# A decoder layer on one core: h's first quads asked for later, one more group with two k tiles by sevens, silu's product behind a split, diff heads closer together

## The chip, the cores and the metric

The kernel runs on one core of a Trainium2 chip, in float32. The metric is the device time of one execution in microseconds (us), the median of several runs. The engines are TensorE (PE; PEld is its weight load), VectorE (DVE), ScalarE (ACT), GpSimd (POOL) and SyncE (SP). SyncE and GpSimd issue DMAs.

## What is computed

One hybrid decoder layer on 256 tokens of width 2048: a half-step SwiGLU FFN, a mixer of two attentions (MLA with 8 heads, differential attention with 4 heads), and a second half-step FFN, each with a residual and a LayerNorm.

```python
def _swiglu(x, w_gate, w_up, w_down):
    return (jax.nn.silu(x @ w_gate) * (x @ w_up)) @ w_down
...
h = _layer_norm(ALPHA * h + 0.5 * _swiglu(h, ffn1_w_gate[l], ffn1_w_up[l], ffn1_w_down[l]), ln1_g[l], ln1_b[l])
mix = _mixer(h, positions, ...)
h = _layer_norm(ALPHA * h + mix, ln2_g[l], ln2_b[l])
h = _layer_norm(ALPHA * h + 0.5 * _swiglu(h, ffn2_w_gate[l], ffn2_w_up[l], ffn2_w_down[l]), ln3_g[l], ln3_b[l])
```

The FFN's inner width is 5632. Its inner activations, silu(gate) * up, are called h below.

## The kernel before

**Products.** A float32 product is made of three passes in the type fp32r. Each operand is split into a high part (a cast on ScalarE, L154) and a low part (a subtraction on VectorE, L155). `triple` (L207 to L210) multiplies high by high, high by low and low by high into one PSUM bank. Weights come by DMA as blocks of 128 x 1024 (two k tiles by 512 columns) on SyncE's queue and are split into pairs of the ring `wring`.

**Units and the order.** The work is a list of units, each with a load, a prep (adds and split) and the products (`unit`, `advance`). A load runs three units ahead of the prep, and preps run four units ahead of the products. `later(n, fn)` emits fn after n more units of products. This sets the order of the program's text. The order on each engine is then set by a scheduler at compile time. It may move an instruction ahead when its data and its buffer are there, it keeps the given order where `tc.issue_after(ins)` asks for it (an edge on the engine of `ins` alone, without a wait of its own), and buffers of one tag are handed out in turn. The activations of all stages share 41 slots of 4 KB per partition (tag "act"), and short-lived tiles share 6 (tag "tmp").

**Gate and up.** `ffn` first makes two column blocks with `project` (16 k tiles in 8 units of 12 matmuls each per block). Then ten groups follow (`Hybrid.group`, p = 1 to 10). A group makes two column blocks, that is one quad of h: 512 columns of h for both halves of the tokens. Inside a group, k tiles 0 to 7 are multiplied by a scheme with seven products in place of eight ("sevens": forms 1, 5, 6, 7, 2, 4, 3), where sums and differences of weight blocks are formed in place in the buffers `sraw` (L428 on VectorE, and L430 as an accumulating DMA on GpSimd). The other k tiles are plain units (L457). In a "wide" group k tiles 8 and 9 go by sevens too: each form has a third piece of 512 columns (buffers `eraw`, activation forms `xe` and `xm` of class `Extra`), and there are six plain units in place of eight:

```python
            elif wide:
                order = "15pp6p72q4q3q"
            elif seeded:
                order = "15pp6p7p2q4q3qq"
```

A digit is a form (three pieces when wide, two otherwise, of 6, 6 and 3 matmuls), and p or q is a plain unit of 12 matmuls. Groups 2 to 9 are wide, group 1 and group 10 are not. A wide group has 177 matmuls of 512 columns, a narrow one 180.

**From the group to h.** `sum_done` adds a snapshot to the bank (`gus`, L885), `half` calls silu on ScalarE (`sg`, L863) and multiplies it with up on VectorE (`hb`, L869), one unit later in the groups' later parts (`wait` is 1 there). Twelve units after a quad's second half, `put_h` transposes it in blocks of 32 (`blocks`, L715) and writes it to DRAM with four DMAs per token half on GpSimd's queue (`turn_out`, L717, into `hT`).

**Back from DRAM.** `get_h(q)` asks for a quad on GpSimd's queue (`hraw`, L893, two DMAs of 256 KB), and `split_h(q)` splits it into `h`. While group 10 is emitted, quads 3, 4 and 0 are asked for (units 3, 6 and 9 of it, counted from seven units before the end of group 9) and quads 3 and 4 are split (units 13 and 16). The down projection (`Sliced`) begins with quads 3 and 4. Quads 0 to 2 go through sevens there (`QuadForms`, tiles `xs` and `f`).

**The diff heads.** After the second hybrid run of the mixer, the four differential heads are spread over the units of the remaining projections. Each has four stages: scores, turn of the probabilities (L1103, L1105), values (L1248 to L1250), turn of the result (L1268). Stage i of head h is emitted at unit 2 + 6h + 3i + i // 3. Between them stand the column projections of q and k of the MLA heads, whose results are turned through DRAM (`turn_to_cols`, copies at L737).

Of the kernel before, what the change touches and what calls it, by code (L numbers as in the profile page):

```python
# [15 lines left out]
ALU = mybir.AluOpType  # L16
# [7 lines left out]
KF = DFF // P  # L24
# [35 lines left out]
def layer_kernel(ctx: ExitStack, tc: tile.TileContext, a: dict, out: bass.AP):  # L60
    nc = tc.nc
    V, S, GP, PE = nc.vector, nc.scalar, nc.gpsimd, nc.tensor
# [13 lines left out]
    def act_tile(shape, dt=F32, name="act"):  # L76
        return apool.tile(shape, dt, tag="act", name=nm(name), bufs=SLOTS)

    def tmp_tile(shape, name="tmp", dt=F32):
        return small.tile(shape, dt, tag="tmp", name=nm(name), bufs=6)  # L80
# [22 lines left out]
    def later(n, fn):  # L103
        uid[0] += 1
        heapq.heappush(todo, (step[0] + n, uid[0], fn))
# [42 lines left out]
            assert (k, b) in self.ready, (self.name, k, b)  # L148
            return self.tiles[k // 8, b][which][:, k % 8, :]

    cast, lows, fetched = [None], [None], [None]

    def split(hi, lo, src):
        cast[0] = S.copy(hi, src)  # L154
# [189 lines left out]
    def behind_split(n):  # L344
        return tc.issue_after(line[-n].ins) if len(line) >= n else nullcontext()
# [366 lines left out]
    def turn_out(row, to):  # L712

        t = tmp_tile([P, 512], "blocks")
        V.transpose(t, row)  # L715
        for i in range(4):
            nc.gpsimd.dma_start(to.rearrange("(g r) (i f) -> i r g f", g=4, i=4)[i],  # L717
                                t[32 * i:32 * (i + 1), :].rearrange("r (g f) -> r g f", g=4))

    def turned(v):  # L720
# [2 lines left out]
    def turn(row, use, wait, more):  # L723
        to = dram.tile([P, 512], F32, name=nm("turn"))
        turn_out(row, to)

        def back():
            t = tmp_tile([P, 512], "turned")
            nc.gpsimd.dma_start(t, to)
            later(more, lambda: use(turned(t)))  # L730
        later(wait, back)
# [120 lines left out]
    def ffn(n, x, wgu, wdn, residual, g, bt, each, first=None, between=None, nxt=None, cols=None, norm=None, pending=None):  # L852
        hb = {}
        hT = dram.tile([KF // 4, 2, P, 512], F32, name=f"hT{n}")

        def put_h(b, q):
            with behind_split(1):
                turn_out(hb[b, q], hT[q, b])

        def half(c, b, up, gate, wait=0):  # L860
            q = c // 2
            sg = tmp_tile([P, 256], "sg")
            S.activation(sg, gate, AF.Silu)  # L863
            if c % 2 == 0:
                hb[b, q] = tmp_tile([P, 512], "hb")
            o = (c % 2) * 256

            def product():
                V.tensor_tensor(out=hb[b, q][:, o:o + 256], in0=up, in1=sg, op=ALU.mult)  # L869
            if wait:  # L870
                later(wait, product)
            else:
                product()
            if c % 2 == 1:
                later(12, lambda: put_h(b, q))
# [4 lines left out]
        def sum_done(c, b, bank, snap, op):  # L880
            if snap is None:
                gu_done(c, b, bank)
                return
            t = tmp_tile([P, 512], "gus")
            V.tensor_tensor(out=t, in0=bank, in1=snap, op=op)  # L885
            half(c, b, t[:, 256:512], t[:, 0:256], 1)
# [2 lines left out]

        def get_h(q):  # L890
            raw = got[q] = act_tile([P, 2, 512], F32, "hraw")
            for b in range(2):
                nc.gpsimd.dma_start(raw[:, b, :], hT[q, b])  # L893

        def split_h(q):
            raw = got.pop(q)
            hq[q] = [act_tile([P, 2, 4, P], F32R, "h") for _ in range(2)]
            for b in range(2):
                split(*(t[:, b].rearrange("p k (i c) -> p k i c", i=4) for t in hq[q]), turned(raw[:, b, :]))
# [31 lines left out]
        for p in range(1, KF // 4):  # L931
            if p == KF // 4 - 1:
                for i, q in enumerate((3, 4, 0)):
                    later(3 + 3 * i, lambda q=q: get_h(q))
                later(13, lambda: split_h(3))
                later(16, lambda: split_h(4))
            hy.group(wgu[2 * p], wgu[2 * p + 1],
                     lambda n, b, bank, snap, op, p=p: sum_done(2 * p + n, b, bank, snap, op),
                     1 < p < KF // 4 - 1, p > 1)
        ln = LayerNorm(0.5, residual, g, bt, each, nxt, cols,  # L940
                       ((24, 26, 48, 50) if pending is None else (13, 14, 60, 62), (94, 97, 100, 103)),
                       35 if cols is None else None, pending, () if pending is None else (17, 32, 67, 82))
# [10 lines left out]
        for p in range(2):  # L953
# [30 lines left out]
            else:  # L984
                call(len(units) - 8, widen)
            down.run(wdn[2 * p], wdn[2 * p + 1], units, forms,
                     lambda m, b, bank, sign, p=p: ln.fold(2 * p + m, b, bank, sign),
                     lambda m, b, bank, p=p: ln.evac(2 * p + m, b, bank), calls, 8 * p)
# [119 lines left out]
    def mixer(x):  # L1108
# [105 lines left out]
        def gate(i, f, hook=None):  # L1214
            project((a["wgm"], a["wgd"])[i][f], x, KD, 512, lambda b, bank: keep_gate(i, f, b, bank), hook=hook)
# [57 lines left out]

        for h in range(DH):
            for i, f in enumerate(diff_head(h)):
                later(2 + 6 * h + 3 * i + i // 3, f)
        gate(1, 2, c_back)
        qT = [cols_proj(a["wuq"][c], cn, 4, "qT") for c in range(2)]
        qrT = act_tile([P, 4, T], F32, "qrT")
# [116 lines left out]

    h1 = Acts(KD, "h1", (0, 1))
    ffn(1, xq, a["gu1"], a["dn1"], a["x"], a["ln1_g"], a["ln1_b"], keep(0), first_tokens, second_tokens, h1, a["ln1_cols"])

    yq = mixer(h1)  # L1400
    h2 = Acts(KD, "h2", (0, 1, 2))
    ln = LayerNorm(1.0, res[0], a["ln2_g"], a["ln2_b"], keep(1), h2, a["ln2_cols"], ((1, 3, 11, 13), ()), 1,
# [94 lines left out]
```

## Time and profile before

| what | value |
|---|---|
| median of three runs | 1974.06 us (1972.81 to 1976.11) |
| the profiled execution | 1972.85 us, its span 1971.1 us |
| granted TensorE clock | 0.998 |
| ScalarE, the commonest group: casts of raw into wring, L154 | 467 instructions, 482.2 us |
| VectorE, the same for the low parts, L155 | 467 instructions, 559.1 us |
| VectorE, adds on sraw, L428 | 168 instructions, 200.2 us |
| GpSimd, writes of h, L717 | 176 instructions, 97.1 us |
| HBM | 246 GB/s over the span |

A row of a timeline gives the start in us from the span's start, the length in us, the engine, the line, the operation, the tiles (out<-in), the shape and the count; in brackets stands how long the engine was idle before it and what ended that. A row of waits gives the total in us, how often, and the longest. A row of the table by stretches gives the length of the stretch and each engine's busy time with the number of its instructions. A row of DMA issues gives the queue, the count, the size and the median us from issue to landing.

### The profile page before, as it was taken

The numbers are of one execution on the slowest core, as the hardware profiler recorded it, in microseconds if no ns is written. First come the engines' busy times: TensorE is split into PE (matmuls) and PEld (weight loads), VectorE is DVE, ScalarE is ACT, GpSimd is POOL, SyncE is SP. The second block draws the span as 40 slices with busy tenths as digits, with TensorE's granted clock in tenths as the row PEclk, the third lists the DMA queues.
The fourth block names the chain that finished last, engine by engine and source line by source line (L and its number), as shares of the span: only waits on it lengthen the run. The fifth ranks groups of instructions, "written<-read, shape, count | busy, mean of one in ns | idle before, by whom it ended". The sixth has DMA issues, their size and how long they took to land.

```text
span 1971.1 us, 25747 instructions
## 1 busy us (share of the span) xinstructions
PE 1955.1 (99%) x8784; PEld 1620.0 (82%) x8784; DVE 1773.5 (90%) x2175; ACT 1265.5 (64%) x1650; POOL 291.0 (15%) x503
## 2 busy tenths in 40 slices
PE   9999999999999999999999999999999999999997
PEld 7888888888888898888888888888888888888886
DVE  7999999999998879988976677789999999999986
ACT  6666767676655566666667765556676776665661
POOL 0112111122100010102223120001211112210000
PEclk9999999999999999999999999999999999999999
DMA  8978888777776666767667668578888878786763
GB/s 309 287 227 262 285 270 251 235 216 281 296 235 222 209 218 254 244 224 259 223 198 241 234 216 271 199 263 254 254 263 294 243 243 249 238 321 237 274 234 124
DMA packets 147478, 485.71 MB, mean 246 GB/s; under 512 B 20961, under 2 KB 21009, under 8 KB 147345
## 3 DMA queue, kind: packets, MB, share of 16 engines
q1 hardware_dynamic: 117360, 397.99, 58.2%
q0 software_dynamic: 29984, 86.07, 16.4%
q8 instruction: 69, 1.13, 0.2%
q14 instruction: 65, 0.52, 0.1%
HBM read 455.13 MB, written 28.84 MB: 246 GB/s over the span
## 4 chain that ended last, share of the span: by engine, by line
PE 95%; DVE 2%; DMA 1%; issue 1%; ACT 0%; SPq 0%; DVEq 0%; ACTq 0%
PE mm L209 30%; PE mm L210 30%; PE mm L208 30%; DVE wring L155 1%; PE tr L208 1%; PE tr L210 1%; PE tr L209 1%; DMA sraw<-in_gu_dram 1%; PE tr L671 0%; DVE sraw L428 0%; ACT wring L154 0%; DMA raw<-in_gu_dram 0%; PE tr L1228 0%; PE tr L1301 0%; PE tr L1303 0%
## 5 line engine op out<-in xcount | busy, mean ns | idle before, releaser
L154 ACT CAST wring<-raw 128x1024 fp32r<-128x1024 f32 (+2 forms) x467 | 482.2, 1038 | 296.5 <-PE mm L210 207.2
L155 DVE TENSOR_TENSOR wring<-raw,wring 128x1024 fp32r<-128x1024 f32 (+2 forms) x467 | 559.1, 1206 | 95.4 <-ACT wring L154 92.8
L154 ACT CAST wring<-sraw 128x1024 fp32r<-128x1024 f32 x436 | 454.8, 1054 | 230.2 <-DVE sraw L428 94.2
L155 DVE TENSOR_TENSOR wring<-sraw,wring 128x1024 fp32r<-128x1024 f32 x436 | 523.2, 1228 | 21.6 <-ACT wring L154 18.8
L210 PE MATMUL mm<-wring,h 128*128 128x512 f32 (+2 forms) x1248 | 480.2, 385 | 0.0
L208 PE MATMUL mm<-wring,h 128*128 128x512 f32 (+2 forms) x1248 | 480.2, 385 | 0.0
L209 PE MATMUL mm<-wring,h 128*128 128x512 f32 (+2 forms) x1248 | 479.8, 385 | 0.0
L209 PE MATMUL mm<-wring,xs 128*128 128x512 f32 x776 | 302.2, 389 | 1.3 <-DVE wring L155 1.3
L208 PE MATMUL mm<-wring,xs 128*128 128x512 f32 x776 | 302.2, 389 | 0.0
L210 PE MATMUL mm<-wring,xs 128*128 128x512 f32 x776 | 302.0, 389 | 0.0
L209 PEld LDWEIGHTS mm<-wring,h 128*128 128x128 f32 x1248 | 234.5, 188 | 46.8 <-DVE wring L155 0.7
L210 PEld LDWEIGHTS mm<-wring,h 128*128 128x128 f32 x1248 | 234.5, 188 | 46.5 <-DVE h L155 0.7
L208 PEld LDWEIGHTS mm<-wring,h 128*128 128x128 f32 x1248 | 234.4, 188 | 46.4 <-ACT h L154 0.6
L428 DVE TENSOR_TENSOR sraw<-sraw,sraw 128x1024 f32<-128x1024 f32 x168 | 200.2, 1229 | 3.5 <-DMA sraw<-in_wdv_dram 1.6
L209 PEld LDWEIGHTS mm<-wring,xs 128*128 128x128 f32 x776 | 145.7, 188 | 32.5 <-DVE wring L155 2.3
L208 PEld LDWEIGHTS mm<-wring,xs 128*128 128x128 f32 x776 | 145.7, 188 | 30.1
L210 PEld LDWEIGHTS mm<-wring,xs 128*128 128x128 f32 x776 | 145.7, 188 | 30.0
L717 POOL DMA_DIRECT2D hT<-blocks x176 | 97.1, 562 | 370.0 <-DVE blocks L715 368.2
L208 PE MATMUL mm<-wring,x 128*128 128x512 f32 x336 | 130.8, 390 | 0.8 <-ACT wring L154 0.8
L209 PE MATMUL mm<-wring,x 128*128 128x512 f32 x336 | 131.0, 390 | 0.5 <-DVE wring L155 0.5
L210 PE MATMUL mm<-wring,x 128*128 128x512 f32 x336 | 130.6, 389 | 0.0
L430 POOL DMA_DIRECT2D sraw<-in_gu_dram x40 | 35.6, 900 | 359.4 <-DVE sraw L428 309.0
(307 smaller groups left out, 2289.6 us busy)
## 6 DMA issues: line engine op xcount, KB each, us to landing
sraw<-in_gu_dram SPq DMA_DIRECT2D x160, 512.0 KB, 5.4
raw<-in_gu_dram SPq DMA_DIRECT2D x159, 512.0 KB, 4.7
raw<-in_dn_dram SPq DMA_DIRECT2D x140, 512.0 KB, 4.7
sraw<-in_gu_dram POOLq DMA_DIRECT2D x40, 512.0 KB, 6.9
sraw<-in_dn_dram SPq DMA_DIRECT2D x36, 512.0 KB, 5.6
hraw<-hT POOLq DMA_DIRECT2D x68, 256.0 KB, 6.2
eraw<-in_gu_dram SPq DMA_DIRECT2D x64, 256.0 KB, 6.0
raw<-in_w_out_dram SPq DMA_DIRECT2D x32, 512.0 KB, 4.3
```

Of the source, the lines that this page charges most:

```text
L154: cast[0] = S.copy(hi, src)
L155: lows[0] = V.tensor_tensor(out=lo, in0=src, in1=hi.bitcast(F32), op=ALU.subtract)
L208: PE.matmul(o, xh, wh, start=first, stop=False, skip_group_check=again)
L209: PE.matmul(o, xh, wl, start=False, stop=False, skip_group_check=again)
L210: PE.matmul(o, xl, wh, start=False, stop=last, skip_group_check=again)
L428: last = V.tensor_tensor(out=R[src][i], in0=R[src][i], in1=R[add[1]][i], op=ALU.add)
L430: nc.gpsimd.dma_start(R["12"][s], source("22", s), accum_op=ALU.add)
L717: nc.gpsimd.dma_start(to.rearrange("(g r) (i f) -> i r g f", g=4, i=4)[i], t[32 * i:32 * (i + 1), :].rearrange("r (g f) -> r g f", g=4))
```

## The change

Four places are touched. `turn_out` keeps its last DMA in `turned_out[0]`, and `get_h` puts its requests behind the one that is the last when the request is emitted, on GpSimd. The product of silu and up, where it is delayed by a unit, is put behind the split that is third from the end of those emitted so far, on VectorE. Group 10 becomes wide. The stages of diff head h are emitted at 2 + 5h + 3i + i // 3.

```diff
-    cast, lows, fetched = [None], [None], [None]
+    cast, lows, fetched, turned_out = [None], [None], [None], [None]
...
-            nc.gpsimd.dma_start(to.rearrange("(g r) (i f) -> i r g f", g=4, i=4)[i],
+            turned_out[0] = nc.gpsimd.dma_start(to.rearrange("(g r) (i f) -> i r g f", g=4, i=4)[i],
                                 t[32 * i:32 * (i + 1), :].rearrange("r (g f) -> r g f", g=4))
...
             def product():
-                V.tensor_tensor(out=hb[b, q][:, o:o + 256], in0=up, in1=sg, op=ALU.mult)
+                with behind_split(3) if wait else nullcontext():
+                    V.tensor_tensor(out=hb[b, q][:, o:o + 256], in0=up, in1=sg, op=ALU.mult)
...
         def get_h(q):
             raw = got[q] = act_tile([P, 2, 512], F32, "hraw")
-            for b in range(2):
-                nc.gpsimd.dma_start(raw[:, b, :], hT[q, b])
+            with tc.issue_after(turned_out[0].ins):
+                for b in range(2):
+                    nc.gpsimd.dma_start(raw[:, b, :], hT[q, b])
...
-                     1 < p < KF // 4 - 1, p > 1)
+                     p > 1, p > 1)
...
-                later(2 + 6 * h + 3 * i + i // 3, f)
+                later(2 + 5 * h + 3 * i + i // 3, f)
```

`behind_split(n)` is `tc.issue_after(line[-n].ins)`, where `line` holds the VectorE halves of the groups' splits in the order in which they were emitted.

## The prediction

> **What bounds the kernel now.** I read the page's head, the waits of TensorE, its timeline, the table by stretches, and last the timelines around TensorE's two stops inside the gate/up groups.
>
> ```profile
> span 1971.1 us, 25747 instructions
> ...
> PE 1955.1 (99%) x8784; PEld 1620.0 (82%) x8784; DVE 1773.5 (90%) x2175; ACT 1265.5 (64%) x1650; POOL 291.0 (15%) x503
> ```
>
> ```profile
> PE mm L209 <- DVE wring L155: 1.8, 4, 0.7
> PE tr L1248 <- ACT pt L1105: 1.1, 1, 1.1
> ...
> PE tr L1103 <- DVE p L1237: 0.2, 1, 0.2
> ```
>
> ```profile
> 229.81 0.39 PE L208 MATMUL mm<-wring,x 128*128 128x512 f32 x1
> ...
> 242.51 0.39 PE L210 MATMUL mm<-wring,xs 128*128 128x512 f32 x1
> ```
>
> TensorE is the bound. Its waits are a few us in all, and between the last two rows lie 57 products: 12.70/56 = 0.227 us from start to start. The 0.39 us of a record overlaps the next one, so a product that goes is worth 0.227. Whatever the change wins is products left out or one of these few waits. What it can lose is larger, because of the engine behind TensorE:
>
> ```profile
> core 0: us, PE busy (x) PEld busy (x) DVE busy (x) ACT busy (x) POOL busy (x), PEclk, DMA share, GB/s
> 217.90:258.90 41.00, 40.27 (x179) 33.04 (x177) 39.06 (x44) 27.47 (x36) 9.20 (x15) 1.00 0.83 271
> 258.90:299.00 40.10, 40.10 (x177) 33.12 (x178) 40.10 (x47) 27.82 (x37) 7.03 (x11) 1.00 0.84 256
> 419.40:460.20 40.80, 40.80 (x181) 33.80 (x181) 37.90 (x47) 26.78 (x35) 8.18 (x15) 1.00 0.73 248
> ```
>
> These are groups 5, 6 and 10 of the first FFN, nearly. In a wide group (6) VectorE is busy all the time; in the last, narrow one it has some 3 us free, ScalarE over a quarter everywhere. VectorE's steps, from the rows below (a record overlaps the next by 0.09): 1.13 us for 1024 columns, 0.60 for 512, 0.33 for 256, 1.22 for a pair of transposes.
>
> ```profile
> 254.27 0.68 DVE L885 TENSOR_TENSOR gus<-mm,snap 128x512 f32<-128x512 f32 x1
> 254.87 1.22 DVE L155 TENSOR_TENSOR wring<-sraw,wring 128x1024 fp32r<-128x1024 f32 x1
> 256.00 0.69 DVE L885 TENSOR_TENSOR gus<-mm,snap 128x512 f32<-128x512 f32 x1
> 256.60 0.42 DVE L869 TENSOR_TENSOR hb<-gus,sg 128x256 f32<-128x256 f32 x1
> ...
> 271.63 1.31 DVE L715 STREAM_TRANSPOSE blocks<-hb 128x512 f32<-128x512 f32 x2
> ```
>
> A wide group: 20 splits of 1024 and 7 of 512 (26.8), adds of 6 x 1.13 + 3 x 0.60 (8.6), three gus, four hb, two transposes (4.3): 39.7 us, against 177 x 0.227 = 40.1 of TensorE. The narrow one: 22 splits, six adds, the same rest: 36.0 against 180 x 0.227 = 40.8. So VectorE regains about 0.4 us per wide group and nearly 5 in the narrow one. What it loses in a wide group stays lost for long.
>
> Now the stop of group 6, and its twin in the second FFN:
>
> ```profile
> 237.20 2.17 POOL L893 DMA_DIRECT2D hraw<-hT  x4 [2.13 <-DMA hT<-blocks]
> ...
> 247.38 1.05 ACT L154 CAST wring<-sraw 128x1024 fp32r<-128x1024 f32 x1 [2.71 <-DMA sraw<-in_gu_dram]
> 248.78 0.42 DVE L869 TENSOR_TENSOR hb<-gus,sg 128x256 f32<-128x256 f32 x1 [1.91 <-ACT sg L863]
> 257.53 1.22 DVE L155 TENSOR_TENSOR wring<-sraw,wring 128x1024 fp32r<-128x1024 f32 x1
> 257.69 0.39 PE L208 MATMUL mm<-wring,xs 128*128 128x512 f32 x1
> 258.81 0.50 PE L209 MATMUL mm<-wring,xs 128*128 128x512 f32 x1 [0.73 <-DVE wring L155]
> ...
> 1531.68 0.39 PE L208 MATMUL mm<-wring,xs 128*128 128x512 f32 x1
> 1532.60 0.50 PE L209 MATMUL mm<-wring,xs 128*128 128x512 f32 x1 [0.53 <-DVE wring L155]
> ```
>
> The two quads 4 and 0 of h (four requests, 1 MB), wanted only by the down projection, are asked for in group 5. The next weights land late: median time to landing of sraw in 236 to 248 us, then in the same phase of the next group:
>
> ```profile
> sraw<-in_gu_dram SPq DMA_DIRECT2D x6, 512.0 KB, 7.0
> ...
> sraw<-in_gu_dram SPq DMA_DIRECT2D x6, 512.0 KB, 5.2
> ```
>
> ScalarE waits 2.71, VectorE 1.91, and ten us later TensorE loses 258.81 - 257.69 - 0.23 = 0.89 us (0.69 in the twin). Its undisturbed lead is read where a split ends and the L209 that needs it starts, at the two tightest units:
>
> ```profile
> 215.54 1.22 DVE L155 TENSOR_TENSOR wring<-sraw,wring 128x1024 fp32r<-128x1024 f32 x1
> 217.80 0.39 PE L209 MATMUL mm<-wring,xs 128*128 128x512 f32 x1
> ...
> 237.83 1.22 DVE L155 TENSOR_TENSOR wring<-sraw,wring 128x1024 fp32r<-128x1024 f32 x1
> 240.92 0.39 PE L209 MATMUL mm<-wring,xs 128*128 128x512 f32 x1
> ```
>
> 1.04 us at form 5, 1.87 at form 4. The first checks the account: 1.91 lost less 1.04 of lead is 0.87, and 0.89 was seen.
>
> **The change, part by part.** *Tenth group wide.* Three products fewer in each FFN: 6 x 0.227 = -1.36 us, sure. [...] The trace steps at 227, and that stands. The price lies on VectorE: 3.7 us more in that group (39.7 - 36.0). ScalarE gets 1.5 splits' worth more and has 14 us free; the requests change by 0.25 MB net, on POOL.
>
> *First quads of h.* At the place in the program where quads 3, 4 and 0 are asked for, the last write of h that has been emitted is that of quad 8 (quad 9's comes some 15 units later). So POOL issues all six requests, 1.5 MB at 0.54 us each, right behind the row at 392.83, from 397.2 on, just where the loads of the next group go out:
>
> ```profile
> 237.23 0.62 ACT L154 CAST h<-hraw 128x512 fp32r<-128x512 f32 x1
> ...
> 384.29 0.74 DVE L155 TENSOR_TENSOR h<-hraw,h 128x512 fp32r<-128x512 f32 x1
> 392.83 4.41 POOL L717 DMA_DIRECT2D hT<-blocks  x8 [14.49 <-DVE blocks L715]
> 398.87 4.63 SPq L420 DMA_DIRECT2D sraw<-in_gu_dram  x4
> ...
> 455.27 0.39 PE L208 MATMUL mm<-wring,h 128*128 128x512 f32 x1
> ```
>
> POOL itself has room, and h is wanted only at 455.27. The old stops go: -0.89 - 0.69 = -1.58. What is late next is the same thing one phase before the tenth group. The burst is half as large again, but starts some 2 us earlier against the weights, since these quads have long been written and need no wait as the 2.13 in the old row. I take the same loss on VectorE, 1.91; bounds 0 (all of it in idle queue time) and 3.0. Behind it stands the tenth group, now without VectorE's free 5 us, and there h's own splits fall: in the old trace ScalarE cast quad 3 at 237 and VectorE could do its half only at 384, when a slot of the last wide group came free; now the slots come free one group later, so all four of 0.60 (2.4 us) land in group 10, ahead of form 4.
>
> So in each FFN: at form 5, 1.91 - 1.04 = 0.9 us of stop. At form 4: what is still owed, 1.04, plus 2.4, less 0.3 regained, less the lead of 1.87: 1.3 us. Together 2.2, twice +4.4. Lower bound: no loss from the burst, 2.4 - 0.3 - 1.87 = 0.2, twice +0.4. Upper: 3.0 - 1.04 + 1.3 = 3.3, twice +6.6.
>
> *Product behind a split.* It goes behind a split two units ahead of the unit that was just multiplied; VectorE in a group is already four ahead by then (the row at 256.60 stands behind the split at 254.87). I cost it at 0; bounds -0.3 and +0.3, one hb of 0.33 on either side of a tight split.
>
> *Diff heads 5 apart.* The last head's scores are traced three units (8.2 us) earlier, its values also.
>
> ```profile
> 1047.44 1.47 PE L1228 MATMUL tr<-dkT,dqT 128*128 128x128 f32 x8
> ...
> 1064.76 1.01 DVE L1084 SCALAR_TENSOR_TENSOR st<-tr,bias 128x384 f32<-128x384 f32 x2
> 1076.22 0.62 ACT L737 COPY kT<-turned 128x512 f32<-128x512 f32 x1 [1.13 <-DMA turned<-turn]
> 1077.69 0.47 ACT L1105 COPY pt<-tr 128x384 f32<-128x384 f32 x1
> ```
>
> Its scores are done at 1049, its softmax starts 16 us later, because the six tmp buffers are handed out in program order and the turns of k stand before it. Then pt queues behind a copy that waits for a DMA, and TensorE waits 1.1 + 0.2. Ahead of the turns of k all of it is over before that copy: -1.3. Bounds: -1.6 (some switching goes too) and +1.3, when the copy's wait falls on a weight cast instead.
>
> **Sum.** -1.36 - 1.58 + 4.4 + 0 - 1.3 = +0.2 us. The profiled execution took 1972.85 around its span of 1971.1, the median of the three runs is 1974.06; 0.2 on the median gives 1974.3.
>
> **Rivals.** *All of it hides.* The early burst uses idle queue time, VectorE finds gaps for h's splits, and the heads give their better bound: -1.36 - 1.58 - 1.6 = -4.5: 1969.5. For it: group 4 had quad 3's two requests without a stop. Against it: the 39.7 of 40.1, and a lower bound above that still has a stop of 0.2.
>
> *VectorE is the bound through the tenth group* (slower). Besides h's 2.4, the first forms of quad 0 (0.33 + 4 x 0.33 + 2 x 0.60 = 2.9) are drawn ahead of form 4. With the burst at 3.0 a stop of 3.3 + 2.9 = 6.2 per FFN, 12.4 - 4.2 = +8.2: 1982.2; with the burst at 1.91, 5.1 twice, +6.0: 1980.0. It decides once what VectorE owes passes the 1.87 of lead. For it: no spare time in group 6; against it: those forms are traced behind the group's splits.
>
> *The queues share evenly.* [...] As a mechanism here: the loss grows with the bytes that stand beside the weights, 1.91 x 1.5 = 2.9, a stop of 3.2 per FFN, 6.4 - 4.2 = +2.2: 1976.2. The two landing times (7.0 and 5.2) agree in direction; the earlier start speaks against it.
>
> *The heads win nothing*, the wait moves to a weight cast: +0.2 + 1.3 = 1975.6, or 1976.9 with the bound.
>
> **How the numbers follow.** Chances: the sum 0.40, sharing 0.08, heads 0.10, all hidden 0.18, VectorE bound 0.24. About 0.2% (3.95 us) is what a measurement can tell: below 1970.1 only the hidden case, 0.18; above 1978.0 only the VectorE case, 0.24; within, 0.58. The forecast's own range is 1971.5 to 1977. The range for 8 in 10 takes in most of the hidden case and the lower half of the slow one: 1969.5 to 1980.5.
>
> **What would show it.** Right: no stop near 257 and 1531; hraw six in a row on POOL behind quad 8's write; TensorE waiting for L155 near 418 and again 20 to 25 us later; the h splits of quads 3 and 4 on VectorE inside the tenth group; no wait of L1248 for pt. Wrong: hraw behind quad 9's or 10's write, other tiles in the freed slots, a wait in the down projection, or kT late for the first MLA scores.

## The result and the profile after

The changed kernel takes 1982.51 us (median; 1979.53 to 1986.79), the kernel before beside it 1974.00 (1972.81 to 1976.11). The ratio is 1.0043, with a 95% interval of 1.0029 to 1.0056: slower by 8.5 us. The forecast was 1974.3, the range 1969.5 to 1980.5, so the time lies outside it. The profiled execution of the changed kernel took 1979.53 us around a span of 1977.8, 6.7 more than the span before. Behind L890 its line numbers are two higher (L1268 is L1270 now), and the product of silu and up stands on L870 (it was L869).

The page's head after, then the first waits of TensorE (total, how often, longest):

```profile
span 1977.8 us, 25757 instructions
...
PE 1955.3 (99%) x8778; PEld 1617.2 (82%) x8778; DVE 1780.6 (90%) x2191; ACT 1262.6 (64%) x1658; POOL 292.6 (15%) x505
```

```profile
PE mm L209 <- DVE wring L155: 5.0, 7, 1.0
PE tr L1270 <- DVE orow L1263: 2.6, 1, 2.6
PE tr L209 <- DVE wring L155: 1.5, 1, 1.5
```

Six matmuls fewer, and yet a longer span. The waits of L209 for a low part went from 1.8 to 5.0 + 1.5 (the second row is the same line with a bank of the tag `tr`, in the down projection). The 1.1 of L1248 for pt is gone, and 2.6 of L1270 for orow stands in its place.

GpSimd's timeline ahead of the tenth group of the first FFN; the median landing times of the weights that go out there, after and then before:

```profile
391.95 4.41 POOL L717 DMA_DIRECT2D hT<-blocks  x8 [14.89 <-DVE blocks L715]
396.36 3.23 POOL L895 DMA_DIRECT2D hraw<-hT  x6
```

```profile
sraw<-in_gu_dram SPq DMA_DIRECT2D x6, 512.0 KB, 8.8
hraw<-hT POOLq DMA_DIRECT2D x6, 256.0 KB, 8.1
```

```profile
sraw<-in_gu_dram SPq DMA_DIRECT2D x6, 512.0 KB, 5.0
```

The six requests stand in a row behind quad 8's write, as predicted, and the weights beside them land after 8.8 us in place of 5.0. What this does to ScalarE, then VectorE, then TensorE (the brackets hold the idle time before):

```profile
409.22 1.05 ACT L154 CAST wring<-sraw 128x1024 fp32r<-128x1024 f32 x1 [3.72 <-DMA sraw<-in_gu_dram]
...
536.09 0.62 ACT L154 CAST h<-hraw 128x512 fp32r<-128x512 f32 x1 [2.46 <-DMA hraw<-hT]
...
548.54 0.62 ACT L154 CAST h<-hraw 128x512 fp32r<-128x512 f32 x1 [4.33 <-DMA hraw<-hT]
```

```profile
410.62 0.42 DVE L870 TENSOR_TENSOR hb<-gus,sg 128x256 f32<-128x256 f32 x1 [3.33 <-ACT sg L863]
...
426.59 0.68 DVE L155 TENSOR_TENSOR h<-hraw,h 128x512 fp32r<-128x512 f32 x1
...
429.46 0.68 DVE L155 TENSOR_TENSOR h<-hraw,h 128x512 fp32r<-128x512 f32 x1
...
432.94 1.28 DVE L155 TENSOR_TENSOR h<-hraw,h 128x512 fp32r<-128x512 f32 x2
...
443.94 0.42 DVE L155 TENSOR_TENSOR xs<-hraw,xs 128x256 fp32r<-128x256 f32 x1
444.28 2.35 DVE L155 TENSOR_TENSOR wring<-sraw,wring 128x1024 fp32r<-128x1024 f32 x2
```

```profile
416.75 0.39 PE L208 MATMUL mm<-wring,xs 128*128 128x512 f32 x1
417.97 0.50 PE L209 MATMUL mm<-wring,xs 128*128 128x512 f32 x1 [0.83 <-DVE wring L155]
...
584.18 0.39 PE L208 MATMUL tr<-wring,xs 128*128 128x512 f32 x1
586.11 0.50 PE L209 MATMUL tr<-wring,xs 128*128 128x512 f32 x1 [1.54 <-DVE wring L155]
```

VectorE lost 3.33 us, more than the upper bound of 3.0, and took h's four splits (2.4 us at the prediction's 0.60 each) inside the tenth group, ahead of form 4, whose split is the row at 444.28. The stop at 584, 1.93 from start to start where 0.23 is due, was in no part of the sum. Its cause stands in ScalarE's rows at 536 and 549: it waits for quads of h that land late, with casts of weights behind it. In the kernel before, its longest wait for h there is this one:

```profile
530.33 0.62 ACT L154 CAST h<-hraw 128x512 fp32r<-128x512 f32 x1 [0.82 <-DMA hraw<-hT]
```

GpSimd's requests in the down projection, after and then before:

```profile
531.19 1.07 POOL L895 DMA_DIRECT2D hraw<-hT  x2 [11.30 <-DVE h L155]
544.36 2.12 POOL L895 DMA_DIRECT2D hraw<-hT  x4 [12.10 <-ACT wring L154]
```

```profile
534.06 1.07 POOL L893 DMA_DIRECT2D hraw<-hT  x2 [7.33 <-DVE h L155]
539.89 1.07 POOL L893 DMA_DIRECT2D hraw<-hT  x2 [4.76 <-PE mm L210]
```

A request can go out only when its slot of the tag "act" has been read for the last time. With the tenth group wide, these two pairs go out together at 544.36, where one went at 534 and one at 540 before. TensorE's work is 2.4 us behind by then, so that is 7.9 and 2.1 us later against the work, while the cast that needs the first of them stands in ScalarE's order at the same place. So what used to be early by a few us now comes just in time or late.

The table by stretches of groups 9 and 10 shows VectorE busy for 40.69 of 40.8 us in the tenth group, where it had some 3 us free:

```profile
378.90:419.90 41.00, 39.90 (x175) 32.39 (x173) 37.50 (x43) 26.73 (x35) 9.54 (x17) 1.00 0.84 278
419.90:460.70 40.80, 39.26 (x169) 31.32 (x170) 40.69 (x50) 29.39 (x39) 8.91 (x16) 1.00 0.64 190
```

In the mixer, TensorE's and ScalarE's timelines after, with VectorE's result of the last head after and before:

```profile
1069.19 0.59 PE L1252 MATMUL tr<-dv,pt 128*128 128x256 f32 x2
1083.94 0.44 PE L1270 MATMUL tr<-ident,orow 128*128 128x128 f32 x2 [2.55 <-DVE orow L1263]
```

```profile
1077.67 1.05 ACT L154 CAST wring<-raw 128x1024 fp32r<-128x1024 f32 x1 [1.97 <-DMA raw<-in_wbd_dram]
1078.62 0.38 ACT L1256 ACTIVATE junk<-tr 128x256 f32<-128x256 f32 x1
```

```profile
1083.40 0.88 DVE L1263 SCALAR_TENSOR_TENSOR orow<-tr,f,subg 128x256 f32<-128x256 f32 x2
```

```profile
1083.98 0.88 DVE L1261 SCALAR_TENSOR_TENSOR orow<-tr,f,subg 128x256 f32<-128x256 f32 x2
```

These times can't be compared as they stand, because the kernel after is 4.6 us behind by then: one and the same product of the projections starts at 998.26 after and at 993.70 before. Against the work, the last head's values are multiplied some 14 us earlier (1069 against 1079). The squares that come next on ScalarE start at 1078.62, behind casts of weights that wait for their DMA, and the result is there at 1083.40 against 1083.98, 5.1 us earlier against the work. TensorE comes to the turn at 1081.4 (1083.94 less its wait of 2.55) against 1084.6, which is 7.8 us earlier against the work. So the result moved less far than its consumer, and TensorE waits for the difference.

Stops of TensorE, as the time from the start of one product of 512 columns to the next less 0.227, summed by place where it is 0.15 or more. The last column is the second profile of the changed kernel (n_after_again, below). "Half clock" is a stretch in which the granted clock of TensorE is about 0.5; the rows of one, at 0.51, are shown at n_after_again.

| place | before | after | after, again |
|---|---|---|---|
| 257 and 1531 (sixth groups) | 1.58 | 0 | 0 |
| tenth group, first FFN | 0 | 3.44 | 4.21 |
| tenth group, second FFN | 0 | 2.12 | 2.61 |
| down projection, first FFN, 560 to 600 | 0 | 1.70 | 2.88, and 1.56 of half clock |
| last diff head, 1074 to 1086 | 1.63 | 2.71 | 2.36 |

With -1.36 for the products, the rows give +5.4 in the first profile (6.7 seen; 0.45 more stands at 950, a wait for dkT) and +9.1 in the second (10.0 seen).

### The profile page after: what moved, and what is told of

Its sections match the earlier page's. It is cut to its first block, busy times and chain, and to the rows that moved or that the text cites. A ratio compares the mean times of both kernels' runs of the same rounds, so it can differ in the third digit from the quotient of the medians.

```text
span 1977.8 us, 25757 instructions
## 1 busy us (share of the span) xinstructions
PE 1955.3 (99%) x8778; PEld 1617.2 (82%) x8778; DVE 1780.6 (90%) x2191; ACT 1262.6 (64%) x1658; POOL 292.6 (15%) x505
## 4 chain that ended last, share of the span: by engine, by line
PE 89%; DVE 5%; DMA 3%; issue 2%; ACT 1%; POOL 0%; SPq 0%; DVEq 0%; ACTq 0%; POOLq 0%
PE mm L209 28%; PE mm L210 28%; PE mm L208 28%; DVE wring L155 2%; DVE sraw L428 1%; DMA sraw<-in_gu_dram 1%; PE tr L209 1%; PE tr L210 1%; PE tr L208 1%; ACT wring L154 1%; PE tr L671 0%; DMA raw<-in_gu_dram 0%; DMA sraw<-in_wdk_dram 0%; DMA sraw<-in_wdv_dram 0%; DMA turn<-blocks 0%
## 5 line engine op out<-in xcount | busy, mean ns | idle before, releaser
L155 DVE TENSOR_TENSOR wring<-raw,wring 128x1024 fp32r<-128x1024 f32 (+2 forms) x463 | 552.2, 1201 | 94.9 <-ACT wring L154 93.2
L209 PE MATMUL mm<-wring,h 128*128 128x512 f32 (+2 forms) x1242 | 477.8, 385 | 0.0
L209 PE MATMUL mm<-wring,xs 128*128 128x512 f32 x776 | 303.1, 391 | 4.3 <-DVE wring L155 4.3
L209 PEld LDWEIGHTS mm<-wring,h 128*128 128x128 f32 x1242 | 233.3, 188 | 46.2 <-DVE wring L155 0.7
L209 PEld LDWEIGHTS mm<-wring,xs 128*128 128x128 f32 x776 | 145.6, 188 | 38.1 <-DVE wring L155 8.4
L209 PE MATMUL mm<-wring,x 128*128 128x512 f32 x330 | 128.8, 390 | 0.9 <-DVE wring L155 0.8
L208 PE MATMUL mm<-wring,x 128*128 128x512 f32 x330 | 128.5, 390 | 0.6 <-ACT wring L154 0.6
L210 PE MATMUL mm<-wring,x 128*128 128x512 f32 x330 | 128.3, 389 | 0.0
```

The lines of the kernel that those rows point to most:

```text
L155: lows[0] = V.tensor_tensor(out=lo, in0=src, in1=hi.bitcast(F32), op=ALU.subtract)
L208: PE.matmul(o, xh, wh, start=first, stop=False, skip_group_check=again)
L209: PE.matmul(o, xh, wl, start=False, stop=False, skip_group_check=again)
L210: PE.matmul(o, xl, wh, start=False, stop=last, skip_group_check=again)
```

## The experiments

Each ratio stands against the kernel before in the same comparison (medians 1972.98, 1973.38, 1973.41, 1973.30, 1973.30 in the five).

**The parts alone.** The edit on silu's product was not run by itself: VectorE's 2191 instructions stand in the same order in the profile of b_wide_tenth, which lacks it, and in that of abc_no_heads, which has it.

a_quads_late keeps only the edge on the requests:

```diff
+            with tc.issue_after(turned_out[0].ins):
```

> The kernel before with the requests for h's first quads behind the last write alone (narrow tenth group, heads 6 apart). Theory (VectorE's free time decides): the stops near 257 and 1531 us go (-1.6); the burst now stands ahead of the narrow tenth group, where VectorE has nearly 5 us free, so at most a stop of 1 us stays at its start and none later: 1972 to 1974 us. Rival (the burst alone costs what it cost, or more, wherever it lands): stops of 1 to 2 us in each FFN at the start of the tenth group, 1974 to 1977. Second rival (slots): the later quads of h are asked for too late in the down projection, and a stop appears there of 1 to 2 us.

b_wide_tenth keeps only the wide group:

```diff
-                     1 < p < KF // 4 - 1, p > 1)
+                     p > 1, p > 1)
```

> The kernel before with the wide tenth group alone (early requests for h, heads 6 apart). Theory (VectorE): six products fewer (-1.4), the old stops stay, and the tenth group, with 3.7 us more on VectorE and the splits of two quads of h, stops TensorE late in the group by 1 to 2 us per FFN: 1974 to 1977 us. Rival (the slots held one group longer push the requests of the later quads, and ScalarE waits for them in the down projection): a stop in the down projection of about 1.7 us in the first FFN, as in the changed kernel near 584 us.

d_heads_5 keeps only the heads:

```diff
-                later(2 + 6 * h + 3 * i + i // 3, f)
+                later(2 + 5 * h + 3 * i + i // 3, f)
```

> The kernel before with the diff heads 5 units apart alone. Theory (the last head's result is paced by the six tmp buffers, whatever its place in the program): the stop moves from the values (1.1 us at L1248) to the turn of the result (2.6 us), plus small ones: +2 us in the span, 1975.5 to 1977 us. Rival (the longer stop also lowers the granted clock in some executions): the runs scatter upward by 2 to 6 us more and their mean clock is 0.996 to 0.997 instead of 0.998.

abc_no_heads is the whole change without that last edit:

```diff
-                later(2 + 5 * h + 3 * i + i // 3, f)
+                later(2 + 6 * h + 3 * i + i // 3, f)
```

> The changed kernel with the heads back at 6 units. Theory: the FFN part alone, -1.6 (old stops) -1.4 (products) +5.6 (stops in the tenth groups) +1.7 (down projection) = +4.3 in the span, 1977.5 to 1979.5 us as a median, with stops of 1.0, 1.2 and 1.0 us in the first FFN's tenth group and 1.0 and 1.0 in the second's. Rival (clock): if the scatter of the changed kernel up to 1986.8 us comes from the mixer's long stop, this one scatters like the kernel before; if it comes from the stops in the FFN, it scatters like the changed one.

| kernel | median | ratio (95%) | stops in its profile |
|---|---|---|---|
| a_quads_late | 1974.52 | 1.0007 (0.9998 to 1.0016) | none at 257, 1531; 1.73 at 416, 1.01 at 1691; 0.61 at 1788 |
| b_wide_tenth | 1977.53 | 1.0018 (1.0007 to 1.0029) | 1.18 at 257, 0.81 at 1538; 0.68 at 442 and at 1723; 2.87 at 581 to 582, then half clock; 2.03 at 1081, then half clock |
| d_heads_5 | 1973.58 | 0.9997 (0.9988 to 1.0006) | 1.51 at 256 to 258, 1.18 at 1534; 3.37 at the last head's turn, then half clock |
| abc_no_heads | 1982.18 | 1.0037 (1.0023 to 1.0051) | 3.57 and 2.15 in the tenth groups; 3.70 at 563 to 586 |

The heads have no share in the loss that can be measured; the edge and the wide group together have nearly all of it, and more together (+9.2 in the medians, +7.3 by the ratio) than one by one (+1.5 and +4.6, by the ratios +1.4 and +3.6), though by the intervals that last difference could be chance. Of the four medians only that of a_quads_late lies where an expectation had it (that of its rival); b_wide_tenth and abc_no_heads are slower than expected, d_heads_5 is faster. The edge does what it says in one place and gives it back in another: the stop moves from 257 to 416 and gets larger.

The stop in the first FFN's down projection comes with the wide group, with the edge or without, and so do the late requests: two pairs go out together in b_wide_tenth, apart in a_quads_late. b, then a:

```profile
542.68 2.12 POOL L893 DMA_DIRECT2D hraw<-hT  x4 [12.81 <-ACT wring L154]
```

```profile
535.77 1.06 POOL L894 DMA_DIRECT2D hraw<-hT  x2 [8.44 <-DVE h L155]
540.76 1.06 POOL L894 DMA_DIRECT2D hraw<-hT  x2 [3.93 <-PE mm L210]
```

In the second FFN the edge alone has a smaller one, the 0.61 at 1788; ScalarE waits 4.99 us for h at 1767 there.

**The down projection.** e_h_split_late takes abc_no_heads and splits each quad of h three units later; the requests stay where they are in the program.

```diff
-                call(first_use, lambda q=q: split_h(q))
+                call(first_use + 3, lambda q=q: split_h(q))
```

> The changed kernel without the heads' edit, and in the down projection each quad of h is split three units (8.2 us) later than it was, while it is asked for at the same unit. Theory (requests for h that come just in time): in the kernel without the heads' edit ScalarE stood 3.18, 0.82 and 4.75 us at its casts of h near 538 and 551, with casts of weights behind them; three units later the data is there, these waits fall under 1 us in all, the stops of TensorE at 585 to 586 (0.74 and 2.10) are gone, and the median falls from 1982.2 to between 1978.5 and 1980.5. Rival (VectorE still owes from the tenth group, and the casts of h only show it): the waits go but a stop of 2 to 3 us stays between 560 and 600, and the median stays within 1 us of 1982.2.

It took 1977.93, 1.0029 (1.0018 to 1.0040). No stop over 0.15 between 455 and 680; ScalarE's longest wait at h's casts from 528 on:

```profile
531.82 0.62 ACT L154 CAST h<-hraw 128x512 fp32r<-128x512 f32 x1 [0.78 <-DVE h L155]
```

The theory held for the stop: the place at which ScalarE, whose casts of weights stand behind it in order, waits for h is what stops TensorE 40 us later. Its worth is less sure: 3.70 in the profiles, 4.3 by the medians, 1.6 by the ratios, with intervals that overlap; the next pair sharpens it.

**The tenth group.** f_group_split_late takes abc_no_heads and emits the two splits there 12 units later, past form 4.

```diff
-                later(13, lambda: split_h(3))
-                later(16, lambda: split_h(4))
+                later(25, lambda: split_h(3))
+                later(28, lambda: split_h(4))
```

> The changed kernel without the heads' edit, and the splits of quads 3 and 4 inside the tenth group are emitted 12 units later, so that VectorE has one of the four halves ahead of form 4 instead of four. Theory (VectorE's debt): 3 x 0.60 = 1.8 us less stand ahead of form 4, so the stops at 444 (0.95) and 1724 (0.96) fall under 0.2 each, those at 416 to 419 and 1699 (burst of requests) stay at 1.0 to 2.5, and the median falls by 1.5 to 2.0, from 1982.2 to 1980.2 to 1980.7, if the down projection takes the 1.8 us. Rival (the debt only moves): the stops at 444 and 1724 go, but 1 to 2 us of new stops appear within 25 us behind them or the one at 585 grows by as much; median within 1 us of 1982.2.

It took 1981.79, 1.0043 (1.0030 to 1.0055): the rival's time. The stops of 0.95 at 444 and 0.96 at 1724 are gone, and the down projection has one of 0.38 and one of 2.10, here TensorE's two rows, with half clock behind them:

```profile
583.42 0.50 PE L208 MATMUL tr<-wring,xs 128*128 128x512 f32 x1 [0.22 <-ACT wring L154]
...
585.74 0.50 PE L209 MATMUL tr<-wring,xs 128*128 128x512 f32 x1 [1.82 <-DVE wring L155]
```

The rival's mechanism is not what the profile shows, though: the stops in the down projection did not grow, they came to 2.48 where abc_no_heads has 3.70, with 0.62 more at 1756 in the second FFN. Over both FFNs the stops are 2.7 us less. Two stretches of 3.4 us at half clock, the one behind 2.10 here (0.53) and one behind 2.49 at 1082 in the mixer (0.51), took that back; the profile of abc_no_heads has none. So whether VectorE's debt from the tenth group is handed on stays open.

ef_both_late has both edits.

> The changed kernel without the heads' edit, with h's splits later in the down projection (three units) and inside the tenth group (12 units). Theory (two debts on VectorE, one after the other: the tenth group's, and that of requests that come just in time): with the second paid, what the first hands on no longer meets a stop, so the stops at 444 (0.94) and 1720 (0.96) go and none comes back at 580 to 590; those of the six requests at once (416 to 419: 2.45; 1693 to 1695: 1.0 to 1.7) stay. From 1977.9 with the down projection alone to 1975.7 to 1976.5. Rival (VectorE is the bound from the tenth group through the down projection, so every stop taken out comes back): a stop of 1 to 3 us between 455 and 600, median 1977.5 or more.

1975.98, 1.0015 (1.0006 to 1.0023), as the theory has it. Against f alone, whose interval begins at 1.0030, the later split in the down projection is worth 5.8 us. That includes the half clock in f. With the splits late in both places no stop is left in the first FFN behind 428. What is left are those of the six requests at once:

```profile
417.94 0.50 PE L209 MATMUL mm<-wring,xs 128*128 128x512 f32 x1 [1.21 <-DVE wring L155]
420.61 0.50 PE L209 MATMUL mm<-wring,xs 128*128 128x512 f32 x1 [1.02 <-DVE wring L155]
...
1695.59 0.50 PE L209 MATMUL mm<-wring,xs 128*128 128x512 f32 x1 [1.01 <-DVE wring L155]
```

**The requests.** g_requests_spread is the kernel before with an edge for each early quad; `written[q]` holds the last write of quad q.

```diff
+        behind_write = {3: 5, 4: 6, 0: 8}
...
-            for b in range(2):
-                nc.gpsimd.dma_start(raw[:, b, :], hT[q, b])
+            w = written.get(behind_write.get(q))
+            with tc.issue_after(w.ins) if w is not None else nullcontext():
+                for b in range(2):
+                    nc.gpsimd.dma_start(raw[:, b, :], hT[q, b])
```

> The kernel before, with one thing changed: quad 3's two requests stand behind the last write of quad 5, quad 4's behind that of quad 6, quad 0's behind that of quad 8 (on GpSimd), so no more than two stand together, in groups six, seven and nine. Theory (the stop comes from four or more requests at once): none of the stops at 257 (0.89) and 1531 (0.69) of the kernel before, none at 416 and 1691 of the kernel with six at once (1.39 and 0.66), and the median falls by 1.2 to 1.6 us against the kernel before. Rival (every request costs the weights its bytes wherever it stands): three smaller stops per FFN, 1.6 us or more in all; median within 0.5 us of the kernel before.

1972.52, 0.9994 (0.9985 to 1.0003). GpSimd asks two at a time, and there is no stop of 0.15 or more from 15 to 680 us and from 1300 to 1950:

```profile
275.28 1.10 POOL L899 DMA_DIRECT2D hraw<-hT  x2 [0.30 <-issue]
...
315.68 1.11 POOL L899 DMA_DIRECT2D hraw<-hT  x2 [0.59 <-ACT snap L386]
...
395.60 1.10 POOL L899 DMA_DIRECT2D hraw<-hT  x2
```

The profile is the theory's; the median fell by 0.9, less than the 1.2 to 1.6 expected, and its interval takes in no change. That fewer than four requests bring no stop is not so in every execution, as p_narrow_again shows below.

**The heads.** h_last_turn_late is d_heads_5 with the last head's fourth stage three units later.

```diff
-                later(2 + 5 * h + 3 * i + i // 3, f)
+                later(2 + 5 * h + 3 * i + i // 3 + (3 if h == 3 and i == 3 else 0), f)
```

> The kernel before with the heads five units apart, and the turn of the last head's result three units later; in TensorE's order it then stands six products (1.4 us) later and in one piece. Theory (the head's result is ready no earlier than before, because its squares stand behind casts of weights whose loads were issued late, so TensorE's wait is only a matter of where the turn stands): the wait of 3.2 us at the turn shrinks by 1.3 to 1.4 to about 1.9, nothing else moves, median 1972.0 to 1972.6 (heads five apart alone: 1973.6). Rival (the split of that result is wanted right behind the turn): the wait moves to the first product that uses it, 3 us in all stay, median 1973.1 to 1974.1.

1970.59, 0.9988 (0.9980 to 0.9997), better than expected. The wait of 3.2 us is 0.50 in the profile, where 1.9 was expected:

```profile
1079.84 0.83 PE L1268 MATMUL tr<-ident,orow 128*128 128x128 f32 x4 [0.50 <-DVE orow L1261]
```

So the wait was a matter of where the turn stood. Two things in the expectation need a correction. The result is ready some 4.5 us earlier than in the kernel before already in d_heads_5 (1079.62 against 1083.98, with the work nearly level), only the turn had moved further. And the heads' own gain in this profile is about 1 us (a stop of 0.66 where the kernel before has 1.63); the stops of the sixth groups, which the edit doesn't touch, happen to be 0.27 in place of 1.58. The wait is not gone either: in the six profiles of the repaired kernels below the stop at this turn is 0.40 to 1.70. m_after_last_turn_late makes the same edit on the changed kernel.

> The changed kernel with the last head's result turned three units later (six products in TensorE's order). Theory (the wait of 2.6 us is only a matter of where the turn stands, and a stop of over 2 us can also cost a stretch at half clock): the stop at the last turn falls from 2.7 to under 1 us, and the median from 1982.5 to 1979 to 1980.5. Rival (the changed kernel's median is set by its FFNs alone): less than 1 us better than 1982.5.

1979.14, 1.0039 (1.0025 to 1.0052). In the medians that is 3.4 less than the change, by the ratios (1.0043 to 1.0039) 0.8, with intervals that overlap; the wait at the last turn is 0.3 in its profile, as the theory has it, and how much of the change's time it was stays unsure.

**What the median has over the first profile.** n_after_again is the changed kernel, for a second profile.

> The changed kernel again, for a second profile. Theory (half clock after long stops): the time is 1981 to 1985, with at least one stretch of 3.4 us at about half the granted clock, behind the stop near 584 or the one near 1081, each worth some 1.7 us, and the same stops as in the first profile within 0.5 us. Rival (other stops that come and go): clock at 1.0 throughout, and stops of 1 us or more at places where the first profile has none.

It took 1982.89 around 1981.1, with the stops at the same places, and the theory's half clock. TensorE's rows, and the table by stretches (its last three columns are the granted clock, the DMA share and GB/s):

```profile
585.77 0.50 PE L208 MATMUL tr<-wring,xs 128*128 128x512 f32 x1 [0.61 <-ACT wring L154]
588.10 0.79 PE L209 MATMUL tr<-wring,xs 128*128 128x512 f32 x1 [1.83 <-DVE wring L155]
588.69 0.63 PE L210 MATMUL tr<-wring,xs 128*128 128x512 f32 x1
589.12 0.63 PE L208 MATMUL tr<-wring,xs 128*128 128x512 f32 x1
```

```profile
584.40:587.80 3.40, 1.26 (x5) 0.48 (x3) 3.40 (x4) 3.13 (x4) 0.00 (x0) 1.00 0.50 177
587.80:591.20 3.40, 3.10 (x7) 2.48 (x8) 3.40 (x4) 0.76 (x1) 0.00 (x0) 0.51 0.86 243
```

Behind a stop of 2.10 the products step at 0.43 us, not 0.227, for 3.4 us: 1.56 us lost on top. Of the six executions behind the median, the one of the first profile has a mean clock of 0.998 (1979.53 us), three have 0.997 (1981.55, 1981.55, 1983.46) and two 0.996 (1983.94, 1986.79). One such stretch takes 3.4 x 0.49 / 1981 = 0.0008 off the mean, which fits one or two of them in the longer executions.

**A version that beats both.** i_spread_wide_late is the kernel before with the tenth group wide, the requests spread as in g, and both edits of ef. k_spread_wide_late_heads adds the heads of h. gh_spread_heads has the edits of g and h alone, the tenth group narrow.

> The kernel before with the tenth group wide and all three repairs: the early requests spread (two at a time behind the last writes of quads 5, 6 and 8), h's splits later in the tenth group and in the down projection. Heads as before. Theory (the three causes are the requests that stand together, h's splits ahead of form 4, and the splits of h in the down projection): no stop over 0.3 us from 200 to 640 and from 1500 to 1950, the six products are won, so 0.89 + 0.69 + 1.36 less than the kernel before at most: median 1970.2 to 1971.2 (0.9984 to 0.9989). Rival (VectorE has no room for a tenth wide group at all): stops of 1 to 3 us in the tenth group or behind it, median 1972.5 to 1975.

> The same with the heads five apart and the last head's result turned six products later. If the parts add up: 1970.7 less the 1.5 to 2.8 that the heads won alone, median 1967.9 to 1969.2 (0.9972 to 0.9979), with no stop over 0.8 us behind the first 15 us. If the heads' gain was chance (its interval reaches from 0.998 to 0.9997): 1970 or more.

> The kernel before, its tenth group narrow, with the early requests spread and the heads five apart with the last turn six products later. Parts added: 1973.2 - 0.9 - 2.0 (bounds -0.5 to -1.6 and -0.6 to -2.8): median 1969.2 to 1971.6. Against the same kernel with the tenth group wide and h's splits late it tells whether the wide group wins its 1.36 us: theory, this one is 1.0 to 1.6 slower; rival, the same or faster.

i took 1973.27, 0.9997 (0.9988 to 1.0005), the rival's time, though the stops that are left in the FFNs are smaller than it said: 0.35 at 297, 0.53 at 418 and 0.66 at 1748. In its profile the time went in the mixer, where the heads are as before: a stop of 2.35 at 1077 with half clock behind it (mean clock 0.997). So its time does not speak for the rival. k took 1970.89, 0.9986 (0.9977 to 0.9994), above what the added parts give because i is, and 2.4 under i, as much as the heads won alone. gh took 1968.96, 0.9977 (0.9968 to 0.9986), and is faster than both kernels. The wide group seemed to lose 1.9 here although its profile had the shorter span. Second profiles and a second comparison followed.

> The repaired kernel with the wide tenth group and the late last turn again, for a second profile. Theory (a wide group leaves VectorE 0.4 us of 40.1, so whatever a transfer is late by, in any wide group, ends as a stop): time near its median of 1970.9, with stops of 0.3 to 1.5 us in the tenth group or in the down projections that the first profile (span 1966.7) didn't have. Rival (the scatter lies elsewhere): no stop over 0.3 us in 200 to 640 and 1500 to 1950, and the difference in the first 15 us or in the mixer.

> The same with the narrow tenth group again. Theory: no stop over 0.3 us in 200 to 640 and 1500 to 1950, as in its first profile; time 1968.2 to 1970.2. Rival: stops there too.

> The repaired kernel with the wide tenth group, once more, beside the narrow one. Theory (no time is left on VectorE in a wide group, so most executions have small stops, the fastest ones none): lowest time at or under that of the narrow one, median 1.0 to 2.0 us above it, with the wider scatter. Rival (the first comparison was chance): median 1.0 to 1.5 us under the narrow one, what six products are worth.

> The repaired kernel with the narrow tenth group, once more. Theory: 0.9970 to 0.9982 of the kernel before, as measured (0.9977), with the smaller scatter of the two. Rival: 0.9985 or more, and the wide one at 0.9980 or less.

o (k again, 1970.26) has stops that the first profile didn't have, two in the down projections:

```profile
PE tr L209 <- DVE wring L155: 1.1, 2, 0.8
```

p (gh again, 1971.66) has one too, of 1.00 at 298 in the seventh group, which the theory did not allow. It stands 22 us behind a pair of requests at 276, as the stop at 257 stood 20 us behind the four at 237, and VectorE's row fits the lead of the prediction, 2.02 - 1.04 = 0.98:

```profile
289.36 0.43 DVE L872 TENSOR_TENSOR hb<-gus,sg 128x256 f32<-128x256 f32 x1 [2.02 <-ACT sg L866]
```

The same place has 0.47 in the later profile of the narrow kernel (VectorE lost 1.49) and 0.35 in that of i (1.38), and there is none in the five other profiles with the requests spread. So two requests at once can still bring a stop. In the second comparison (q is the wide one, r the narrow one) the two are alike: 1969.73, 0.9979 (0.9971 to 0.9988) for the wide one, 1969.72, 0.9981 (0.9972 to 0.9990) for the narrow one. The wide one scatters more (1967.81 to 1971.67 against 1968.64 to 1970.80), but the 1.9 did not come back, and the theory's 1.0 to 2.0 did not either. The six products of the wide tenth group buy nothing that these comparisons can tell, even with its stops repaired; why not is open.

## Why the prediction was wrong

**Six products, -1.36.** Right as a count; it was spent again by what follows.

**Old stops gone, -1.58.** Right, in every kernel with the requests moved or spread. Their size is that of one execution: with the requests where they were, the two come to 1.99 in b, 2.69 in d and 0.27 in h.

**Tenth groups, +4.4.** Right in place and mechanism, mis-sized: +5.6 in the first profile, +6.8 in the second. The term that failed is the loss from the burst in the first FFN, taken as 1.91 because the requests start earlier against the weights; it measured 3.33, beyond the upper bound. Less the lead of 1.04 that is 2.3, and the first FFN's two stops at form 5 are 0.99 + 1.18. The earlier start won nothing; half as many bytes again made the loss 1.74 times as large. It was not one execution's chance: the loss in the first FFN is 3.05 to 4.10 in the eight profiles with six requests at once, and 1.31 to 2.45 in the four with four at the old place. In the second FFN of the first profile VectorE lost 1.85 in three pieces and the stop at form 5 was 1.00, so there the term was about right; in the second profile it lost 2.80. The step is that of the rival "the queues share evenly" (2.9). The weights' 8.8 us beside six requests (9.1 in a_quads_late), 7.0 beside four and 5.0 beside none agree with it in direction; how the queues share the engines no run shows. Form 4 was about right: 0.96 in each FFN against 1.3.

**The down projection, 0.** The sum had no term for it, and "a wait in the down projection" stood only in the list of what would make it wrong. The prediction followed the freed slots as far as h's splits of quads 3 and 4 and stopped there. The later quads' requests are delayed too, and a cast in order on ScalarE turns that into 1.7 to 2.9 us of stop, up to 4.4 with the clock. b shows that the wide group alone brings the late requests and the stop, e that the stop goes when the split stands three units later. That the requests wait for the slots held one group longer is read from the code and the brackets, and was not tested by itself.

**Product behind a split, 0.** Right: it changes no order on VectorE.

**Heads, -1.3.** Wrong in sign in the profile (+1.1 and +0.7), nothing in the median (0.9997). The step that failed is "ahead of the turns of k all of it is over": the values and pt were, but the squares behind them queue on ScalarE behind casts that wait for their weights. So the result came 5.1 us earlier against the work and its turn on TensorE 7.8, and TensorE waits 2.6. The stated bound of +1.3 named a wait on a weight cast; the wait was on orow. h shows that a gain is there (-2.8 by the medians, -2.4 by the ratio, about 1 at the heads in the profile) once the turn stands where the result is.

**What put the time outside the range.** No single step. In the first profile the heads miss their term by 2.4, the down projection by 1.7 and the tenth groups by 1.2; in the second it is 2.0, 4.4 and 2.4. With the down projection repaired (e, heads as before) or with the heads' turn repaired (m), the median lies inside the range.

**The rivals.** The time is that of "VectorE is the bound through the tenth group" (1980.0 to 1982.2) plus 0.3, but not by its price: of quad 0's forms a single split of 0.33 stood ahead of form 4 (the row at 443.94), the stops in the tenth group came to 5.6 to 6.8 and not 10.2 to 12.4, and the rest came in the down projection, in the mixer and from the clock. So that the time is near this rival's is chance, and f leaves open what it said of VectorE's debt.

## What to carry to other kernels

When buffers of one tag are handed out in turn, an edit that holds some of them longer can move later requests that get one of these slots (here two pairs, by 7.9 and 2.1 us against the work): follow the slots to the last of them, and look at the engine that takes its work in order where the data lands. A burst of requests that was moved cost no less than before, and more with its size (in the first FFN 1.91 us on VectorE with four requests, 3.33 with six); taken apart, two at a time, it cost little or nothing in most profiles, and 1 us in one. A stage moved earlier on one engine wins only if its last step, on its slowest engine, moves as far as what consumes it (here 5.1 us against 7.8). Move the consumer to where the result is, not to where its first part is. And compare the times of two profiles against the work done, since one of them may be some us behind.

## What the runs showed of the hardware that was not expected

In the middle of the kernel a stop of TensorE of 2.10 us is in some profiles followed by a stretch of 3.4 us at about half the granted clock: 0.51 from 587.80 to 591.20 in n_after_again (its row stands with that run, 1.56 us lost on top) and 0.53 from 586.10 to 589.50 in f_group_split_late. In the 3.4 us ahead of these TensorE was busy for 1.26 us (the row at 584.40 there) and for 1.36.

The length of the stop alone doesn't decide. The same 2.10 at 586 in abc_no_heads has no such stretch behind it, and neither has the wait of 2.55 at 1081.4 in the first profile of the changed kernel. The granted clock stays at 1.00 in both; abc_no_heads first, then the changed kernel:

```profile
583.22:586.63 3.41, 2.79 (x11) 1.69 (x9) 3.41 (x5) 1.66 (x2) 0.00 (x0) 1.00 0.46 154
586.63:590.04 3.41, 1.64 (x7) 1.38 (x8) 3.41 (x4) 2.23 (x3) 0.00 (x0) 1.00 0.78 251
```

```profile
1080.00:1090.00 10.00, 7.45 (x38) 6.01 (x37) 7.06 (x17) 7.73 (x12) 0.55 (x1) 1.00 0.81 297
```

So a stop of one and the same length costs 1.56 us more in one execution and nothing more in another. What decides between the two was not shown.
